# SiLU-gated product on one core: computed in place, 16 rows to a partition, products packed over rows already read

## The chip, the core and the metric

One core of a Trainium2 chip runs the kernel alone. The metric is device time in microseconds (us) of one execution, as the median of several runs. DVE is VectorE, ACT is ScalarE, SP is SyncE. DMA transfers are issued from two queues, SP's and ACT's, and both are carried out by the core's 16 DMA engines.

## The reference

The input x is float32 of shape 32 x 512 x 2048: 16384 rows of 2048 numbers (8 KiB a row, 134.22 MB). Each row is cut into two halves of 1024, and the output (67.11 MB) is

```python
half_dim = x.shape[-1] // 2
x1, x2 = (x[..., :half_dim].copy(), x[..., half_dim:].copy())
silu_x1 = x1 * (1 / (1 + np.exp(-x1)))
return (silu_x1 * x2).astype(np.float32)
```

Nothing is summed over rows or columns: it is an elementwise stream, two numbers in for one out.

## The kernel before

The rows are cut into 16 tiles of 128 partitions x 8 rows. In a tile a partition takes 8 neighbouring rows, 64 KiB in one piece of memory. `load(i)` (L82, issued on SP) brings a whole tile into `xt`, from a pool of two buffers of 64 KiB a partition. `silu` (L86, on ACT) reads the first halves of the rows and writes a second tile, `ot`, from a pool of two buffers of 32 KiB a partition. `mul` (L93, on DVE) multiplies `ot` in place by the second halves of `xt`. The store (L112, issued on ACT) sends `ot` out, 32 KiB a partition in one piece. The four buffers take 192 KiB of a partition.

The order is written out by hand (`manual_schedule`); waits are put in by the framework from what each instruction reads and writes. Tiles 0 and 1 are loaded ahead; the first load is moved in front of the program's first barrier. After the store of tile i has been queued, `load(i + 2)` is queued on SP. It goes into the buffer that tile i was read from, so it waits for the multiply of tile i. SiLU of tile i writes the output buffer that tile i - 2 left from, so it waits for the store of tile i - 2.

Three places differ from the rest:
- Tile 0 is computed in four chunks of two rows (`KC_EDGE`), and its store is cut into the five pieces of `OPENING`: every fourth partition's first two rows, and so on, growing from 256 KiB to 2 MiB.
- Tile 15, the last, is computed in two chunks of four rows (`KS`) and stored in two pieces (L120).
- L146 is the end of the program: barriers and waits for the last stores.

A transfer is carried out as one packet per partition, and each of the 16 DMA engines takes 8 of the 128 partitions. A DMA engine takes packets in turn from the two queues as long as both have some.

Of the kernel before, what the change touches and what calls it, by code (L numbers as in the profile page):

```python
# [1 line left out]

# [4 lines left out]


def issue_ahead_of_the_first_barrier(nc):

    head, body = nc.main_func.blocks[:2]
    load = next(ins for ins in body.instructions if type(ins).__name__ == "InstDMACopy")
    at = next(
        j for j, ins in enumerate(head.instructions)
        if ins.engine == load.engine and type(ins).__name__ == "InstDrain"
    )
    body.instructions = [ins for ins in body.instructions if ins.name != load.name]  # L20
    head.instructions = head.instructions[:at] + [load] + head.instructions[at:]


@with_exitstack
def kernel(
    ctx: ExitStack,
    tc: tile.TileContext,
    x: bass.AP,
    out: bass.AP,
):  # L30

    nc = tc.nc
    P = nc.NUM_PARTITIONS

    x_flat = x.flatten_outer_dims()  # L40
    out_flat = out.flatten_outer_dims()
    num_rows, in_cols = x_flat.shape
    half = in_cols // 2
    dt = x_flat.dtype

    K = 8
    KC_EDGE = 2
    KS = 4
    OPENING = [
        (slice(0, None, 4), slice(0, 2)),  # L50
        (slice(2, None, 4), slice(0, 4)),
        (slice(2, None, 4), slice(4, None)),
        (slice(0, None, 4), slice(2, None)),
        (slice(1, None, 2), slice(None)),
    ]
    PLAN = [K] * (num_rows // (P * K))

    in_pool = ctx.enter_context(tc.tile_pool(name="in_pool", bufs=2))
    out_pool = ctx.enter_context(tc.tile_pool(name="out_pool", bufs=2))

    plan = []
    row = 0
    for k in PLAN:
        plan.append((row, k))
        row += P * k
    assert row == num_rows
    n_tiles = len(plan)

    def view(flat, i):
        row0, k = plan[i]  # L70
        return flat[row0:row0 + P * k].rearrange("(p k) d -> p k d", k=k)

    nc.at_finalize(issue_ahead_of_the_first_barrier)


    ctx.enter_context(tc.manual_schedule())

    loaded = {}

    def load(i):  # L80
        xt = in_pool.tile([P, K, in_cols], dt, name="xt")
        nc.sync.dma_start(out=xt[:, :plan[i][1], :], in_=view(x_flat, i))  # L82
        loaded[i] = xt

    def silu(ot, xt, c, ce):
        nc.scalar.activation(  # L86
            out=ot[:, c:ce, :],
            in_=xt[:, c:ce, :half],
            func=mybir.ActivationFunctionType.Silu,
        )  # L90

    def mul(ot, xt, c, ce):
        nc.vector.tensor_mul(  # L93
            out=ot[:, c:ce, :],
            in0=ot[:, c:ce, :],
            in1=xt[:, c:ce, half:],
        )

    load(0)
    load(1)  # L100
    for i in range(n_tiles):
        xt = loaded.pop(i)
        ov = view(out_flat, i)
        ot = out_pool.tile([P, K, half], dt, name="ot")
        if i < n_tiles - 1:
            kc = KC_EDGE if i == 0 else K
            for c in range(0, K, kc):
                silu(ot, xt, c, c + kc)
                mul(ot, xt, c, c + kc)

            for ps, ks in OPENING if i == 0 else [(slice(None), slice(None))]:
                nc.scalar.dma_start(out=ov[ps, ks], in_=ot[ps, ks])  # L112
            if i + 2 < n_tiles:
                load(i + 2)
            continue
        for c in range(0, K, KS):
            silu(ot, xt, c, c + KS)
            mul(ot, xt, c, c + KS)
        for c in range(0, K, KS):
            nc.scalar.dma_start(out=ov[:, c:c + KS], in_=ot[:, c:c + KS])  # L120


# [1 line left out]
_INS = ['x']  # L124
_OUTS = [((32, 512, 1024), 'float32')]


# [23 lines left out]
```

## Time and profile before

| | |
|---|---|
| time, median of 3 runs | 470.3 us (470.26 to 470.54) |
| span of the profiled execution, first to last instruction | 468.4 us |
| lying around the span (median less span) | 1.9 us |
| HBM read / written | 134.22 MB / 67.11 MB |
| DVE busy | 139.3 us, 20 multiplies |
| ACT busy | 114.1 us, 20 SiLUs and one table load |
| SiLU / multiply of a whole tile (128 x 8192) | 7.03 us / 8.69 us |
| SiLU / multiply of two rows (128 x 2048) | 1.90 us / 2.29 us |

The span is measured by the profiler within one execution; the time of a run holds what lies around it too. No separate time of the profiled execution is given, so its span stands beside the median of the runs. The profile names idle time by what ended it ("<-DMA out_dram<-ot": the engine waited for a store of `ot` to land). A chain of waits is followed back from the last instruction. Besides the page, the trace holds a record of each DMA packet, with its queue, size, start and duration; times of packets below are counted from the start of the span as well.

### The profile page before, as it was taken

Reading aid. Unit: us, or ns where it says so; the run is one execution under the profiler, and the core shown is the slowest. Engines: PE = TensorE matmul, PEld = TensorE weight load, DVE = VectorE, ACT = ScalarE, POOL = GpSimd, SP = SyncE. Lnnn points to the kernel's source line nnn. Section 1 sums busy time; section 2 is a strip of 40 time slices with the busy share of each in tenths; the row PEclk is TensorE's granted clock in tenths of the full one; section 3 lists DMA queues with packets and bytes.
Section 4 is the critical chain, followed back from the end, with each engine's and each line's share of the span. In section 5 each row is a group of like instructions: output and inputs, shape, how many; then the busy total and the mean of one; then the engine's idle time right before and its main releaser. Section 6 shows DMA issues by size and latency. Waiting matters only on the chain.

```text
span 468.4 us, 185 instructions
## 1 busy us (share of the span) xinstructions
DVE 139.3 (30%) x20; ACT 114.1 (24%) x21; POOL 0.2 (0%) x4
## 2 busy tenths in 40 slices
DVE  0070600704207042070520605116061150602543
ACT  1142305005050050601406014060230602306060
POOL 0000000000000000000000000000000000000000
DMA  9899999999999999999999999899999899999998
GB/s 442 364 470 425 448 403 403 493 403 403 448 465 431 403 442 409 493 403 414 437 448 448 403 448 465 386 448 439 411 493 442 372 439 493 403 448 403 428 423 358
DMA packets 4880, 201.33 MB, mean 430 GB/s; under 512 B 592, under 2 KB 592, under 8 KB 592
## 3 DMA queue, kind: packets, MB, share of 16 engines
q1 hardware_dynamic: 2304, 134.22, 66.4%
q10 hardware_dynamic: 2576, 67.11, 33.2%
HBM read 134.22 MB, written 67.11 MB: 430 GB/s over the span
## 4 chain that ended last, share of the span: by engine, by line
DMA 72%; DVE 14%; ACT 11%; DVEq 1%; issue 0%
DMA out_dram<-ot 63%; DVE ot L93 14%; ACT ot L86 11%; DMA xt<-in_x_dram 9%; DVEq L146 1%
## 5 line engine op out<-in xcount | busy, mean ns | idle before, releaser
L93 DVE TENSOR_TENSOR ot<-ot,xt 128x8192 f32<-128x8192 f32 (+2 forms) x20 | 139.3, 6983 | 321.1 <-ACT ot L86 321.1
L86 ACT ACTIVATE ot<-xt 128x8192 f32<-128x8192 f32 (+2 forms) x20 | 112.8, 5661 | 340.2 <-DMA out_dram<-ot 305.8
L86 ACT ACT_TABLE_LOAD x1 | 1.3, 1283 | 0.8 <-PEq L135 0.8
L135 POOL MEMSET const-bfloat16-1.0<- 128x1 bf16 x1 | 0.1, 102 | 0.0
L135 POOL MEMSET const-uint8-127<- 128x1 uint8 x1 | 0.1, 102 | 0.0
L135 POOL MEMSET const-float32-1.0<- 128x1 f32 x1 | 0.1, 99 | 0.0
L135 POOL MEMSET const-float32-0.0<- 128x1 f32 x1 | 0.1, 98 | 0.2 <-issue 0.2
## 6 DMA issues: line engine op xcount, KB each, us to landing
out_dram<-ot ACTq DMA_DIRECT2D x14, 4096.0 KB, 42.2
out_dram<-ot ACTq DMA_DIRECT2D x3, 2048.0 KB, 6.9
out_dram<-ot ACTq DMA_DIRECT2D x2, 512.0 KB, 17.6
out_dram<-ot ACTq DMA_DIRECT2D x1, 768.0 KB, 28.2
xt<-in_x_dram SPq DMA_DIRECT2D x16, 35.1
out_dram<-ot ACTq DMA_DIRECT2D x1, 256.0 KB, 11.3
```

The costliest lines, as they stand in the source:

```text
L86: nc.scalar.activation(out=ot[:, c:ce, :], in_=xt[:, c:ce, :half], func=mybir.ActivationFunctionType.Silu,)
L93: nc.vector.tensor_mul(out=ot[:, c:ce, :], in0=ot[:, c:ce, :], in1=xt[:, c:ce, half:],)
L135: nc = _bacc.Bacc("TRN2", target_bir_lowering=False, num_devices=1)
L146: with _tile.TileContext(nc) as tc:
```

## The change

Tiles are taken in pairs. A partition now takes 16 neighbouring rows (128 KiB in memory), and there are 8 pairs. The first 8 rows of each partition are loaded into `a` (two buffers of 64 KiB), the other 8 into `b` (one buffer of 64 KiB): 192 KiB as before, and no output buffers. SiLU writes over the first halves that it reads. The multiply writes its products packed, over the front of `a`: `o` is a view of `a` as 16 rows of 1024. The products of a's own rows go to o's rows 0 to 7, those of b's rows to o's rows 8 to 15. A whole pair leaves as one store of 64 KiB a partition.

The half `a` is computed whole, the half `b` in four chunks of two rows. The loads are queued on SP as a(0), b(0), a(1), and then, after each pair's store, b(j+1) and a(j+2). b(j+1) goes where b(j) was read from, so it waits for the last multiply of b(j). a(j+2) goes where o of pair j leaves from, so it waits for every store of pair j.

The stores: pair 0 in five pieces (`OPENING`, now up to 64 KiB a partition), pairs 1 to 4 whole, pair 5 in two halves of the partitions (`HALVES`, even and odd), pair 6 as the rows of `a` and then the rows of `b`, pair 7 as the rows of `a` and then two quarters. In the changed kernel the loads of `a` are at L74, those of `b` at L79, SiLU at L83, the multiply at L88 and the stores at L96.

```diff
-    K = 8
-    KC_EDGE = 2
-    KS = 4
+    K = 8
+    KB = 2
+    PAIR = 2 * K
...
+    WHOLE = [(slice(None), 0, PAIR)]
+    HALVES = [(slice(0, None, 2), 0, PAIR), (slice(1, None, 2), 0, PAIR)]
     OPENING = [
-        (slice(0, None, 4), slice(0, 2)),
-        (slice(2, None, 4), slice(0, 4)),
-        (slice(2, None, 4), slice(4, None)),
-        (slice(0, None, 4), slice(2, None)),
-        (slice(1, None, 2), slice(None)),
+        (slice(0, None, 4), 0, 2),
+        (slice(2, None, 4), 0, 4),
+        (slice(2, None, 4), 4, PAIR),
+        (slice(0, None, 4), 2, PAIR),
+        (slice(1, None, 2), 0, PAIR),
     ]
...
-    in_pool = ctx.enter_context(tc.tile_pool(name="in_pool", bufs=2))
-    out_pool = ctx.enter_context(tc.tile_pool(name="out_pool", bufs=2))
+    a_pool = ctx.enter_context(tc.tile_pool(name="a_pool", bufs=2))
+    b_pool = ctx.enter_context(tc.tile_pool(name="b_pool", bufs=1))
...
+    x_of = x_flat.rearrange("(n p k) d -> n p k d", p=P, k=PAIR)
+    out_of = out_flat.rearrange("(n p k) d -> n p k d", p=P, k=PAIR)
+    a_of, b_of = {}, {}
+    def load_a(j):
+        a = a_pool.tile([P, K, in_cols], dt, name="a")
+        nc.sync.dma_start(out=a, in_=x_of[j, :, :K])
+        a_of[j] = a
+    def load_b(j):
+        b = b_pool.tile([P, K, in_cols], dt, name="b")
+        nc.sync.dma_start(out=b, in_=x_of[j, :, K:])
+        b_of[j] = b
+    def compute(t, o, r0, c, ce):
         nc.scalar.activation(
-            out=ot[:, c:ce, :],
-            in_=xt[:, c:ce, :half],
+            out=t[:, c:ce, :half],
+            in_=t[:, c:ce, :half],
             func=mybir.ActivationFunctionType.Silu,
         )
         nc.vector.tensor_mul(
-            out=ot[:, c:ce, :],
-            in0=ot[:, c:ce, :],
-            in1=xt[:, c:ce, half:],
+            out=o[:, r0 + c:r0 + ce, :],
+            in0=t[:, c:ce, :half],
+            in1=t[:, c:ce, half:],
         )
+    def store(j, o, pieces):
+        for ps, r, re in pieces:
+            nc.scalar.dma_start(out=out_of[j, ps, r:re], in_=o[ps, r:re])
+    load_a(0)
+    load_b(0)
+    load_a(1)
+    for j in range(n_pairs):
+        a, b = a_of.pop(j), b_of.pop(j)
+        o = a.rearrange("p k (h d) -> p (k h) d", h=2)
+        last = j == n_pairs - 1
+        split = j >= n_pairs - 2
+        compute(a, o, 0, 0, K)
+        if split:
+            store(j, o, [(ALL, 0, K)])
+        for c in range(0, K, KB):
+            compute(b, o, K, c, c + KB)
+        if last:
+            store(j, o, [(ALL, K, K + K // 2), (ALL, K + K // 2, PAIR)])
+            break
+        if split:
+            store(j, o, [(ALL, K, PAIR)])
+        else:
+            store(j, o, OPENING if j == 0 else HALVES if j == n_pairs - 3 else WHOLE)
+        load_b(j + 1)
+        if j + 2 < n_pairs:
+            load_a(j + 2)
```

More of the change, by code (lines that the diff above doesn't have):

```diff
@@ L46 @@
     K = 8
-    KC_EDGE = 2
-    KS = 4
-    OPENING = [
-        (slice(0, None, 4), slice(0, 2)),
-        (slice(2, None, 4), slice(0, 4)),
-        (slice(2, None, 4), slice(4, None)),
-        (slice(0, None, 4), slice(2, None)),
-        (slice(1, None, 2), slice(None)),
-    ]
-    PLAN = [K] * (num_rows // (P * K))
-    in_pool = ctx.enter_context(tc.tile_pool(name="in_pool", bufs=2))
-    out_pool = ctx.enter_context(tc.tile_pool(name="out_pool", bufs=2))
[L61 to L71, printed above, removed]
+    KB = 2
+    PAIR = 2 * K
+    n_pairs = num_rows // (P * PAIR)
+    assert n_pairs * P * PAIR == num_rows
+    WHOLE = [(slice(None), 0, PAIR)]
+    HALVES = [(slice(0, None, 2), 0, PAIR), (slice(1, None, 2), 0, PAIR)]
+    OPENING = [
+        (slice(0, None, 4), 0, 2),
[3 more added lines that the diff above has]
+        (slice(1, None, 2), 0, PAIR),
+    ]
@@ L73 @@
+    ALL = slice(None)
+    a_pool = ctx.enter_context(tc.tile_pool(name="a_pool", bufs=2))
+    b_pool = ctx.enter_context(tc.tile_pool(name="b_pool", bufs=1))
     nc.at_finalize(issue_ahead_of_the_first_barrier)
     ctx.enter_context(tc.manual_schedule())
[L78 to L85, printed above, removed]
+    x_of = x_flat.rearrange("(n p k) d -> n p k d", p=P, k=PAIR)
@@ L89, in silu @@
             func=mybir.ActivationFunctionType.Silu,
         )
-    def mul(ot, xt, c, ce):
         nc.vector.tensor_mul(
-            out=ot[:, c:ce, :],
-            in0=ot[:, c:ce, :],
-            in1=xt[:, c:ce, half:],
-        )
[L99 to L120, printed above, removed]
+            out=o[:, r0 + c:r0 + ce, :],
```

## The prediction

> **What bounds the kernel now.** I read the page first, for who is busy.
>
> ```profile
> span 468.4 us, 185 instructions
> ...
> DVE 139.3 (30%) x20; ACT 114.1 (24%) x21; POOL 0.2 (0%) x4
> ...
> DMA  9899999999999999999999999899999899999998
> ...
> q1 hardware_dynamic: 2304, 134.22, 66.4%
> q10 hardware_dynamic: 2576, 67.11, 33.2%
> ```
>
> The two compute engines are busy for 30% and 24%. The two DMA queues, loads (q1) and stores (q10), together hold the 16 DMA engines for 66.4 + 33.2 = 99.6% of the span: 311.0 and 155.5 us. So the bound is the DMA engines' own time, and the only room is 0.4% of 468.4 us, about 2 us. Nothing can make this kernel much faster; what can be lost is continuity. In the packet records, every engine takes its packets back to back, one per partition and transfer: 64 KiB of load in 2.418 us, 32 KiB of store in 1.213, 16 KiB in 0.611, 8 KiB in 0.309. From about 1.9 us after the span's start to its last microsecond no engine pauses for more than 0.1 us.
>
> Then the timeline, at both ends, for the latencies that a pause would be made of.
>
> ```profile
> 21.75 5.51 ACT L86 ACTIVATE ot<-xt 128x2048 f32<-128x2048 f32 x3 [19.70 <-DMA xt<-in_x_dram]
> ...
> 26.02 0.55 ACTq L112 DMA_DIRECT2D out_dram<-ot  x1
> ...
> 32.62 0.33 SPq L82 DMA_DIRECT2D xt<-in_x_dram  x1
> ...
> 439.57 0.34 ACTq L112 DMA_DIRECT2D out_dram<-ot  x1
> 448.01 7.12 ACT L86 ACTIVATE ot<-xt 128x4096 f32<-128x4096 f32 x2 [17.20 <-DMA out_dram<-ot]
> 451.66 8.76 DVE L93 TENSOR_TENSOR ot<-ot,xt 128x4096 f32<-128x4096 f32 x2 [12.13 <-ACT ot L86]
> 456.12 4.67 ACTq L120 DMA_DIRECT2D out_dram<-ot  x2
> ```
>
> Three numbers come out. (a) The first load is issued at 0.00 and its SiLU starts at 21.75, while its eight packets per engine need 8 x 2.418 = 19.34: a load put on drained queues costs 2.41 us beyond its bytes, about 0.38 of it notice (the last packet of a store ended at 447.62, the SiLU waiting for it started at 448.01). (b) The first of the last two stores is issued at 456.12, and its packets start at 456.97: 0.85 us from issue to packet when an engine has just run dry. (c) Four chunks of two rows need 32.62 - 21.75 = 10.87 us from a landed load to an issue behind the last multiply; two chunks (the second store at 28.22) need 6.47.
>
> Last, the chain and the SP queue's waits: who waits for stores today.
>
> ```profile
> DMA out_dram<-ot 63%; DVE ot L93 14%; ACT ot L86 11%; DMA xt<-in_x_dram 9%; DVEq L146 1%
> ```
>
> ```profile
> SPq L82 <- DVE ot L93: 301.6, 14, 23.0
> SPq L82 <- DMA xt<-in_x_dram: 102.9, 14, 20.6
> ```
>
> The chain runs through stores only because SiLU waits for a free output buffer. A load never waits for a store: it waits for the multiply that frees its input buffer (301.6 us in 14 waits), and at that time the next load is already queued. That is why neither queue runs dry.
>
> **The change, part by part.**
>
> *Compute.* Each pair has one SiLU of 7.03, one multiply of 8.69, and four chunks of 1.9 and 2.29 on its second half: ACT 8 x (7.03 + 7.6) = 117 us, DVE 8 x (8.69 + 9.14) = 143 us, against 114 and 139. Both have two thirds of each 58 us pair free, so I cost the extra at nothing; in place, the operands' sizes are the same. If that cover were gone it would be 3 to 4 us.
>
> *Bytes and packets.* Bytes do not change. Store packets per engine fall from 140 to 92 (opening 12, four whole stores 8 each, halves 8, split pairs 16 and 24). Two of 32 KiB cost 2.426 us, one of 64 KiB 2.418: 8 ns each. Packets overlap their neighbours by 3 ns (a tile's period is 29.00 us, its packets sum to 29.05), so 48 x 5 ns, a gain of 0.3 us. The bound: 48 x 8 ns, 0.4.
>
> *The new wait.* Load a(j+2) reuses the buffer that store j leaves from, so on SP it waits for a whole store to land, and b(j+2) stands behind it. On ACT the stores wait as before; behind them stand SiLUs of loads that land later. What matters is whether the load queue runs out before store j has landed.
>
> *Steady state: hidden.* Store j starts 0.38 + 10.87 + 0.85 = 12.1 us after b(j) has landed, while a(j+1) loads. Five of its packets are through by then and one or two more go ahead (the store issued at 26.02 started at 31.02, behind a packet of 28.3). The engines then alternate one store, one load packet, and a transfer's completion write takes a turn too (the before trace shows two loads or two stores in a row at exactly those places). Store j has 9 turns; loads left are one or two packets of a(j+1), eight of b(j+1) and two completions, 11 or 12. So two or three load packets, 4.8 to 7.2 us, remain when the store lands, and the next load needs 1.3 to 2.4. Free, with at least 2.4 us to spare.
>
> *First pair: not hidden.* a(0), b(0), a(1) are queued at once, b(0) lands at 21.4 + 19.3 = 40.7. The opening store is in five pieces: 12 packets and 5 completions, 17 turns. Its first two pieces need only the first half's product, but stand on ACT behind b(0)'s SiLUs: issued near 45, on the engines near 48; the rest follows at 40.7 + 0.4 + 10.9 = 52. From 48 the loads have five packets of a(1), eight of b(1) and two completions, 15 turns. So loads run out first, by one or two store packets, and a(2) may not be issued until the last piece has landed. The next store needs b(1)'s chunks and comes at about 106. So both queues drain. When: 32 load packets (77.4 us), 19.4 us of store, 2.0 us of start: 98.8, or up to 0.8 more, since loads beside the first small stores took 2.5 to 2.75 us in the before trace. The pause is notice plus restart: at least 0.38 + 0.03 + 0.85 = 1.3 us (row b, a store), at most 2.4 (row a, a load, but the program's first). Neither is nearer, so the middle: **1.9 us**, once. It ends the program that much later, because all else is bytes.
>
> *The tail.* Stores after b(7): the first quarter needs 0.38 + 6.47 + 0.85 = 7.7 us. By the same turns, six or seven packets of the preceding half store (1.213 each, 7.3 or 8.5 us) are still queued. A pause of 0.4 us or none; I take none. The last quarter needs 12.1 us, and 7.3 + 4.9 are queued.
>
> *Sum.* 1.9 - 0.3 + 0 = +1.6 us on the profiled span, 468.4 to 470.0. The median of the runs, 470.3, lies 1.9 us above the span for what is around it; that does not change. 470.3 + 1.6 = **471.9 us**.
>
> *A rule that speaks against the change.* In the before trace partitions are read at a pitch of 64 KiB and written at 32 KiB, and all packets but the opening's run at 2.418 and 1.213 us; the change doubles both pitches, and no row shows it for long transfers, but the opening stores (every fourth partition, 128 KiB apart) ran at the usual 0.309 and 0.611 us. The Trainium skill, "DMA: Bandwidth & Descriptors", section "Latency and other measured facts", says that large power-of-two pitches between partitions' rows slow HBM copies: 207 GB/s at 512 KiB where 214 is full. If that 3.3% reached the loads here, an estimate from that page would be 311 x 0.033, some 10 us more; this trace shows none of it.
>
> **The rivals.**
>
> *The pause is hidden (not slower).* If the opening pieces finish at least one 64 KiB packet earlier in the order of turns, a(2) is issued while b(1) still loads. It decides at two turns: the margin is 15 against 17. For it: ACT may issue the first pieces earlier than 45. Against: they cannot come before b(0) lands, and an earlier start brings the ends level rather than reversed. Time: 470.3 - 0.3 = 470.0, no change.
>
> *Faster.* Both the pause and the 0.8 us of slow loads beside the small first stores go: 470.3 - 0.3 - 0.8 = 469.2. Nothing points to it.
>
> *Longer pitch slows packets (much slower).* One per cent on each packet is 4.7 us: 475. Against: the 128 KiB opening stores above.
>
> *The pause recurs.* If a store of 64 KiB packets gets less than its turn, the load queue drains in pairs 1 to 5 also: 5 x 1.9 more, 481. Against: 2.4 us to spare and a fair alternation in the before trace.
>
> **How the numbers follow.** Forecast 0.72, hidden 0.11, faster 0.05, longer pitch 0.08, recurring 0.04. Around the forecast: pause 1.3 to 2.4, packets -0.4 to -0.3, tail 0 to 0.4, opening -0.8 to +0.4. The ends that I keep are 1.3 - 0.4 - 0.8 = +0.1 and 2.4 - 0.3 + 0.4 + 0.4 = +2.9: 470.3 rounded down to 470.2 to take in part of the hidden case, and 473.2. A measurement here tells 0.2%, 0.94 us, from no change. The hidden case and the low corner of the forecast fall within it, so: faster 0.05, same 0.17, slower 0.78.
>
> **What would show it.** Right: one wait of SP for out, ending at 99 to 100, then one pause of 1.3 to 2.4 us in which both queues are empty, seen as one lower digit in the DMA row near a fifth of the span; 64 KiB packets still at 2.418; the other a loads issued 4 to 8 us before the b load ahead of them lands; last SiLU group near 451. Wrong: a DMA row without a gap and a span under 468.8 (hidden), shares of q1 above 311 us (pitch), or gaps at each 58 us (recurring).

## The result, and the profile after

The changed kernel takes 483.3 us (median of 6 runs, 481.5 to 483.8) against 470.3 us: a ratio of 1.0252, 95% interval 1.0225 to 1.0280. I had forecast slower, but by 1.6 us and not by 13.0. The profiled execution took 483.4 us with a span of 481.6, 13.2 us more than the span before. Some executions of a kernel come out over 1.5% longer than its fastest; the ratios here and below leave these out.

The page of the changed kernel (busy tenths of the DMA engines in 40 slices of 12 us; then the two queues' packets, MB and share of 16 engines' span):

```profile
span 481.6 us, 203 instructions
...
DMA  9998989969999999999999999999999999999978
...
q1 hardware_dynamic: 2304, 134.22, 65.9%
q10 hardware_dynamic: 1728, 67.11, 32.3%
```

One slice, 96 to 108 us, is down to six tenths: the forecast pause. But the shares do not fall as a pause of 1.9 us would make them. 65.9% of 481.6 us is 317.4 us of load packets, against 311.0 before: the same 2304 packets with the same bytes took 6.4 us longer on each engine. That part was not in the forecast.

The SP queue's waits of the changed kernel (us in total, times, longest), then its timeline around the pause and at the end (start, us, engine, line, operation):

```profile
SPq L74 <- DMA out_dram<-a: 270.6, 9, 43.5
```

```profile
41.16 1.91 ACT L83 ACTIVATE b<-b 128x2048 f32<-128x2048 f32 x1 [12.32 <-DMA b<-in_x_dram]
41.17 1.20 ACTq L96 DMA_DIRECT2D out_dram<-a  x2
...
52.02 1.81 ACTq L96 DMA_DIRECT2D out_dram<-a  x3
...
102.15 7.31 ACT L83 ACTIVATE b<-b 128x2048 f32<-128x2048 f32 x4 [30.33 <-DMA b<-in_x_dram]
102.24 0.33 SPq L74 DMA_DIRECT2D a<-in_x_dram  x1
...
113.02 0.36 ACTq L96 DMA_DIRECT2D out_dram<-a  x1
...
462.52 7.31 ACT L83 ACTIVATE b<-b 128x2048 f32<-128x2048 f32 x4 [21.37 <-DMA b<-in_x_dram]
...
468.99 4.74 ACTq L96 DMA_DIRECT2D out_dram<-a  x2
```

b(1) and the opening store have landed at the same time, at 101.7, and only then is a(2) issued, at 102.24. The last b half lands at 462.2 and its first store follows 6.47 us after its SiLU has begun, as row (c) had it.

Stretches of the changed kernel (length, then busy time of DVE, ACT and POOL, clock, DMA share, GB/s):

```profile
96.00:104.00 8.00, 0.00 (x0) 1.85 (x2) 0.00 (x0) 1.00 0.72 270
...
114.00:122.00 8.00, 0.00 (x0) 0.00 (x0) 0.00 (x0) 1.00 0.88 319
122.00:172.00 50.00, 14.58 (x4) 14.34 (x5) 0.00 (x0) 1.00 1.00 435
```

The second row is what I had no term for. Nothing computes, both queues have work, store 1 has just been issued, and the rate is 319 GB/s; in the 50 us behind it it is 435. In the packet records all 16 engines have one load packet there, begun at 116.0 to 116.5, that takes 3.3 to 3.9 us instead of 2.418; behind it their first packet of store 1 follows.

From the packet records I made a ledger for each run, in us per engine (sums over all packets divided by 16; "load excess" is the duration of the load packets above 2.418 us for 64 KiB, 1.213 for 32 KiB; idle times are those of the engines between packets; the records name no engine, and an engine's packets are told by each beginning where the one before ended):

| kernel | load excess | idle 4 to 120 us | idle 120 to 440 us | idle from 440 us to the last packet |
|---|---|---|---|---|
| before | 1.42 | 0.02 | 0.05 | 0.18 |
| changed | 7.79 | 4.04 | 0.35 | 2.61 |

The differences, 6.4 + 4.0 + 0.3 + 2.4 us, with 0.2 us less of store packets, make 12.9 of the 13.2 us. The rest, 0.3, I leave unassigned.

### The profile page after: what moved, and what is told of

The parts are those of the page before. It is cut to its first block, busy times and chain, and to the rows that moved or that the text cites. A ratio compares the mean times of both kernels' runs of the same rounds, so it can differ in the third digit from the quotient of the medians.

```text
span 481.6 us, 203 instructions
## 1 busy us (share of the span) xinstructions
DVE 140.7 (29%) x40; ACT 116.0 (24%) x41; POOL 0.2 (0%) x4
## 3 DMA queue, kind: packets, MB, share of 16 engines
q1 hardware_dynamic: 2304, 134.22, 65.9%
## 4 chain that ended last, share of the span: by engine, by line
DMA 70%; DVE 12%; another core or an unknown queue 9%; ACT 5%; DVEq 0%; ACTq 0%; issue 0%
DMA b<-in_x_dram 38%; DMA out_dram<-a 19%; DMA a<-in_x_dram 13%; DVE a L88 12%; ACT a L83 3%; ACT b L83 2%; DVEq L146 0%; ACTq L96 0%; ACTq L83 0%
## 5 line engine op out<-in xcount | busy, mean ns | idle before, releaser
L88 DVE TENSOR_TENSOR a<-a 128x8192 f32<-128x8192 f32 x8 | 69.5, 8692 | 187.0 <-ACT a L83 187.0
L88 DVE TENSOR_TENSOR a<-b 128x2048 f32<-128x2048 f32 x32 | 71.2, 2286 | 145.6 <-ACT b L83 145.6
L83 ACT ACTIVATE b<-b 128x2048 f32<-128x2048 f32 x32 | 58.5, 1897 | 199.9 <-DMA b<-in_x_dram 199.9
L83 ACT ACTIVATE a<-a 128x8192 f32<-128x8192 f32 x8 | 56.2, 7029 | 153.2 <-DMA a<-in_x_dram 153.2
```

Source lines behind the costliest of these rows:

```text
L83: nc.scalar.activation(out=t[:, c:ce, :half], in_=t[:, c:ce, :half], func=mybir.ActivationFunctionType.Silu,)
L88: nc.vector.tensor_mul(out=o[:, r0 + c:r0 + ce, :], in0=t[:, c:ce, :half], in1=t[:, c:ce, half:],)
```

## The experiments

**Which parts count: pair 1 split (e1_split1), all pairs split (e2_splitall), the old order at the new pitch (e3_pitch), the old order with small load packets (e4_load32).**

Pair 1 in two row halves, so that the store queue has work while a(2) waits:

```diff
-        split = j >= n_pairs - 2
+        split = j == 1 or j >= n_pairs - 2
```

> The changed kernel, with pair 1 stored in two row halves (the first right behind the multiply of its a half) instead of whole; all else as changed. The store queue then has work at 99 us, while a(2) waits for the opening store. Theory A (continuity: the 13.2 us more of span are the pause at 99 to 103 us, 4.0 us and 0.75 us of slow first packets behind it; about 5.3 us of load packets that run above 2.418 us when a store starts on an empty store queue; and about 2 us of idle engines before the last two stores): the pause goes and with it one store start, so 5 to 6 us less, 477 to 479 us. Theory B (addresses: loads are slower because a partition's rows lie 128 KiB apart): the pause goes, the slow load packets stay just as many, 478 to 480 us, and they are not tied to store starts. If the pause were the whole loss: 470 to 472 us.

Measured: 476.2, 478.2 and 479.7 us, and 483.6 in the profiled run (ratio of the first three 1.0153, 1.0112 to 1.0194). The pause is gone: 0.16 us of idle time from 4 to 120 us against 4.04. The slowed loads are not: the load excess of the profiled run is 9.97 us, where theory A had it fall. That run took 4 to 7 us longer than the other three, which left no packet records, so how much those lost to slowed loads is not shown. By their times, against 483.3, the pause was worth about 5 us, and was not the whole.

All pairs in row halves:

```diff
-        split = j >= n_pairs - 2
+        split = True
```

> The changed kernel, with every pair stored in two row halves of 32 KiB a partition, each behind its own multiply (pair 0 too, in place of its five pieces); loads and their 128 KiB pitch as changed. Store packets are 32 KiB against 64 KiB of load, so the store queue should never run empty. Theory A: no pause, no store starts, so load packets near 2.418 us throughout (sum above nominal 1 to 2 us an engine, as before the change); what is left is a wait of 1.8 to 2.5 us before the last two stores; 471.5 to 474 us. Theory B: the slow load packets stay, 475 to 479 us.

Measured: 472.75 us (472.1 to 473.3; ratio 1.0044, 1.0026 to 1.0063). Its page, and its timeline at the end:

```profile
span 470.9 us, 200 instructions
...
DMA  9899999998999999999999999999999999999998
```

```profile
452.43 7.31 ACT L83 ACTIVATE b<-b 128x2048 f32<-128x2048 f32 x4 [21.86 <-DMA b<-in_x_dram]
...
458.90 4.74 ACTq L96 DMA_DIRECT2D out_dram<-a  x2
```

In place computing, the 16-row layout, the two-row chunks and a(j+2)'s wait for a store are all still there, and 10.6 of the 13.0 us are gone. The load excess is 2.83 us; from 110 us on no load packet is slow. What is left is two places: 1.08 us of load and 0.4 us of store excess at 100 to 109 us, where the load queue has just run empty and a(2) is issued beside running stores, and 0.98 us of idle before the last stores.

The kernel before, with the pitch of the changed one:

```diff
-        row0, k = plan[i]
-        return flat[row0:row0 + P * k].rearrange("(p k) d -> p k d", k=k)
+        j, t = divmod(i, 2)
+        pair = flat[j * P * 2 * K:(j + 1) * P * 2 * K]
+        return pair.rearrange("(p t k) d -> t p k d", t=2, k=K)[t]
```

> The kernel before, with its order, chunks, buffers and packet sizes, but its tiles laid out as halves of 16-row groups: a partition's loads lie 128 KiB apart (64 before) and its stores 64 KiB apart (32 before). Theory A: nothing changes, 470.0 to 470.7 us. Theory B: several us slower, 475 to 482 us.

Measured: 470.32 us (10 runs; ratio 0.9993, 0.9972 to 1.0014), load excess 1.43 us. Theory B is out: 128 KiB between a partition's loads and 64 KiB between its stores cost nothing. The Trainium skill's rule on large power-of-two pitches ("DMA: Bandwidth & Descriptors", "Latency and other measured facts") does not reach down to these pitches; no run here tried its own, 512 KiB and more.

The kernel before, with loads of 32 KiB a partition:

```diff
-        nc.sync.dma_start(out=xt[:, :plan[i][1], :], in_=view(x_flat, i))
+        for c in range(0, K, 4):
+            nc.sync.dma_start(out=xt[:, c:c + 4, :], in_=view(x_flat, i)[:, c:c + 4])
```

> The kernel before, each load issued as two loads of 4 rows (32 KiB a partition), stores as before. Load and store packets now are of one size, so stores get every second turn and half of the engines' time beside loads instead of a third: the store queue runs empty in each tile and starts anew 14 times beside loads, as in the changed kernel, at the old pitch and with 32 KiB store packets. By the order of turns alone the end has a pause of about 4.6 us (the stores have run out when the last load lands), and 128 more packets an engine cost 0.6 us: 475 to 476 us with load packets at their nominal 1.213 us (theory B, and theory C: that only 64 KiB store packets disturb loads). Theory A: on top of that 0.3 to 1.1 us of slowed load packets at each of the 14 starts, 479 to 490 us.

Measured: 474.1 to 474.4 us in three runs, 479.6 in the profiled one (ratio 1.0101, 1.0045 to 1.0158). The store queue did run empty in every tile, but the load excess is only 3.33 us for 14 starts. Theory A as I had put it, that a store starting on an empty queue costs 0.3 to 1.1 us each time, fails here: it came to that at two of the 14 starts, with 0.45 and 0.95 us.

**Is a start enough? The remedy (e6_fix), bare streams with 64 KiB and 32 KiB stores (m1_starts64, m2_starts32), and 32 KiB stores in the changed kernel (e5_rows).**

All pairs split, with two edits more:

```diff
-        compute(a, o, 0, 0, K)
+        for c in range(0, K, KB if j == 0 else K):
+            compute(a, o, 0, c, c + (KB if j == 0 else K))
...
-            store(j, o, [(ALL, K, K + K // 2), (ALL, K + K // 2, PAIR)])
+            store(j, o, [(ALL, r, r + KB) for r in range(K, PAIR, KB)])
```

> All pairs stored in row halves, as in the run with every pair split (472.75 us), with two more edits. Pair 0's a half is computed in chunks of two rows, so that its first store is issued at about 32.6 us instead of 37.6 and the store that a(2) waits for lands before the load queue runs out. The last b half is stored in four pieces of two rows, each behind its own multiply, so that the first is issued 1.9 us earlier. Theory A' (what costs is a queue that runs empty and starts anew beside the other one, whichever of the two it is, about 1 us of slowed packets each time, and idle engines): the slow packets at 100 to 109 us (1.45 us) and the idle 1 us before the last stores go, 470.0 to 471.0 us. Rival (in place computing or the two-row chunks cost something of their own): it stays at 472 to 473 us.

Measured: 470.87 us against 470.57 of the kernel before in the same set (ratio 0.9997, 0.9981 to 1.0013). Its timeline:

```profile
33.28 0.37 ACTq L96 DMA_DIRECT2D out_dram<-a  x1
...
95.28 0.33 SPq L74 DMA_DIRECT2D a<-in_x_dram  x1
102.74 7.31 ACT L83 ACTIVATE b<-b 128x2048 f32<-128x2048 f32 x4 [22.11 <-DMA b<-in_x_dram]
```

The first store leaves at 33.28, and a(2) is now issued 7.5 us before b(1)'s SiLU instead of just behind it. Load excess 1.60, idle 0.01 and 0.07 us up to 440. So computing in place is as fast as the kernel before once the queues are kept fed, and not faster: the bytes bound both.

The bare stream (the loop of the changed kernel replaced; `s` is a constant tile; the second differs only in storing the first 8 rows):

```diff
+    for i in range(2 * n_pairs):
+        xt = tiles.pop(i)
+        nc.scalar.activation(
+            out=s[:, 0, 0:1] if i % 2 else w,
+            in_=xt[:, 0, 0:1],
+            func=mybir.ActivationFunctionType.Silu,
+        )
+        if i % 2:
+            nc.scalar.dma_start(out=out_of[i // 2], in_=s)
+        if i + 2 < 2 * n_pairs:
+            tiles[i + 2] = load(i + 2)
```

> A bare stream with the changed kernel's transfers: 16 loads in two buffers at the 128 KiB pitch and 8 stores of 64 KiB a partition, of a constant tile; of the computing only one element per partition and load is left, so that store j is issued when load 2j+1 has landed. No load waits for a store, so the load queue never runs empty, but each of the first 7 stores starts on an empty store queue beside loads. Without a cost of starting: 468.4 + about 1.5 us of pause before the last store, - 0.3 us, so some 471.5 us with load packets at 2.418 us. Theory A': 0.5 to 1.3 us of slowed load packets at most of the 7 starts, 475 to 480 us. If the slowed packets need the compute engines' work at the same time: none.

> The bare stream with stores of 32 KiB a partition: only the first 8 of a pair's 16 rows are stored, so half of the output is left out. Bytes take 309.5 + 77.6 us an engine, and without a cost of starting the time is some 393 to 394 us. Theory A' (the start costs, not the store's packet size): the 7 starts cost 0.5 to 1.3 us each as with 64 KiB, 397 to 402 us. Theory C (only store packets of 64 KiB disturb loads): nothing, 393 to 394 us.

Measured: 477.2 us (476.4 and 478.1) and 397.5 us. Both times lie in the range of theory A', but not for its reason. At the first start the loads lost 0.96 and 1.01 us; at the other six 0.01 to 0.13 us with 64 KiB and 0.03 to 0.42 with 32 KiB. Most of what cost time was that the engines drifted apart. In the 64 KiB stream the first load landed on its last engine 0.65 us after its first, the 15th load 14.1 us, the last load 6.5 us; and the last store could not be issued before the slowest engine was done, 6.1 us of idle time per engine. So a start on an empty queue is not sufficient, nor does it take store packets of 64 KiB: theories A' and C both fail.

Pairs 1 to 4 with both row halves stored behind the last multiply:

```diff
-    WHOLE = [(slice(None), 0, PAIR)]
+    WHOLE = [(slice(None), 0, K), (slice(None), K, PAIR)]
```

> The changed kernel with pairs 1 to 4 stored as two stores of 32 KiB a partition, both behind the pair's last multiply (one store of 64 KiB before). By the order of turns each store of a pair now needs 18 turns where 11 or 12 of the loads are left, so the load queue runs dry in pairs 0 to 4, and a(j+2) waits for the store: five pauses of 1.3 to 4 us where the changed kernel has one, each followed by a slow first load packet of about 0.75 us. Theory A': 488 to 500 us. Theory C (64 KiB store packets are what costs): fewer slowed load packets, faster than the changed kernel, below 481 us.

Measured: 490.9 to 492.8 us, 499.0 in the profiled run (ratio 1.0436, 1.0398 to 1.0474). The page:

```profile
span 497.2 us, 212 instructions
...
DMA  9999999989999799998998969898799999999987
```

In this profiled run, 6 to 8 us above the other three, the notches stand 60 us apart, one for each of pairs 0 to 4; the idle time from 120 to 440 us is 14.9 us, and the load excess 10.06 us. Stores of 32 KiB are not a remedy by themselves: with twice the turns they land too late, and the loads wait. The count of turns was right here.

**What a start needs beside it: the changed kernel's waits without its computing, with a long and a short chain (m3_late, m4_early), and a free load queue with the long chain (m5_late_free).**

In each loop `act(w, w)` stands between the landed b half and the store, six times or twice:

```diff
+        act(a[:, 0, 0:1], a[:, 0, 0:1])
+        act(w[:, 0:1], b[:, 0, 0:1])
+        for _ in range(6):
+            act(w, w)
+        act(a[:, 0, 0:1], w[:, 0:1])
+        nc.scalar.dma_start(out=out_of[j], in_=a.rearrange("p k (h d) -> p (k h) d", h=2))
...
-        for _ in range(6):
+        for _ in range(2):
```

> The changed kernel's transfers, buffers and waits (b(j+1) after b(j) has been read, a(j+2) after store j has landed, stores of 64 KiB a partition, all whole), without its computing: what is stored is x as it was loaded, so the output is not the product. Between a landed b(j) and store j stands a chain of six small activations on a scratch tile, 11 to 12 us, as long as the changed kernel's chunks. By the order of turns a(j+2) is then ready 2 to 4 us before the load queue would run out. Theory D (a store that starts on an empty queue slows loads by about 1 us when the load queue has only just been handed its next transfer, and hardly when that was queued long before): 0.5 to 1.3 us of slowed load packets at most of stores 1 to 6, as in the changed kernel, 484 to 489 us. Theory E (the slowed loads need the multiplies and SiLUs of the changed kernel beside them or before them): below 0.2 us at a start but the first, 482 to 483 us.

> The same with two small activations in the chain instead of six: store j is issued 4 to 5 us after b(j) has landed, and a(j+2) is ready some 10 us before the load queue would run out. Theory D: below 0.2 us of slowed loads at each start but the first, 475 to 477 us. If the slowing belongs to a start on an empty store queue alone, or to the buffers and waits: as much as with six activations, 0.5 to 1.3 us a start, 479 to 484 us.

The bare stream with the long chain ahead of each store, where a load only waits for the load that had its buffer:

```diff
+            for _ in range(6):
+                nc.scalar.activation(out=v, in_=v, func=mybir.ActivationFunctionType.Silu)
+            nc.scalar.activation(out=s[:, 0, 1:2], in_=v[:, 0:1], func=mybir.ActivationFunctionType.Silu)
             nc.scalar.dma_start(out=out_of[i // 2], in_=s)
```

> The bare stream with 64 KiB stores of a constant tile (no load waits for a store, each load is queued a whole transfer ahead), now with the chain of six small activations between a landed load and its store, 12 us. Stores so start on an empty queue as late as in the run with the long chain, but the load queue always has its next transfer long before. Theory D (the margin with which the load queue is handed its next transfer decides): below 0.2 us of slowed loads at each start but the first. Theory F (the place decides: a store that starts 12 us into a load, whatever the loads wait for): 0.4 to 1.5 us at most starts, as with the long chain before. The time of the whole says little, since the last store is issued 12 us after the last load: 484 to 492 us.

Measured: 498.7, 484.7 and 490.7 us. From the timelines, one pair each of the changed kernel, of the long and of the short chain: the issue of a(4), the first read of the landed b(3), the store behind it.

```profile
218.53 0.33 SPq L74 DMA_DIRECT2D a<-in_x_dram  x1
223.34 7.31 ACT L83 ACTIVATE b<-b 128x2048 f32<-128x2048 f32 x4 [27.59 <-DMA b<-in_x_dram]
...
234.21 0.36 ACTq L96 DMA_DIRECT2D out_dram<-a  x1
```

```profile
216.26 0.33 SPq L74 DMA_DIRECT2D a<-in_x_dram  x1
221.03 0.20 ACT L103 ACTIVATE w<-b 128x1 f32<-128x1 f32 x1 [31.78 <-DMA b<-in_x_dram]
...
233.14 0.34 ACTq L115 DMA_DIRECT2D out_dram<-a  x1
```

```profile
210.24 0.33 SPq L74 DMA_DIRECT2D a<-in_x_dram  x1
220.61 0.20 ACT L103 ACTIVATE w<-b 128x1 f32<-128x1 f32 x1 [26.77 <-DMA b<-in_x_dram]
...
224.96 0.34 ACTq L115 DMA_DIRECT2D out_dram<-a  x1
```

The lead, from a's issue to the read of the landed b, is 4.8 us in the first two and 10.4 in the third. With the load excess around each start (packets that begin from 6 us ahead of the first store packet to 2.5 us behind it):

| run | lead of the next load, us | load excess at each start after the first, us |
|---|---|---|
| changed kernel, stores 1 to 5 | none, 7.3, 4.8, 4.2, 4.9 | 1.13, 0.02, 0.76, 1.23, 0.54 |
| long chain, stores 1 to 6 | 4.8, 2.8, 4.8, 3.2, 4.4, 2.7 | 0.43, 1.15, 1.57, 1.11, 1.39, 0.93 |
| short chain, stores 1 to 6 | 12.1, 12.1, 10.4, 11.2, 12.1, 11.0 | 0.04, 0.01, 0.04, 0.15, 0.01, 0.06 |
| free load queue, long chain, stores 1 to 6 | a whole load or more | 0.19, 0.00, 0.01, 0.04, 0.04, 0.08 |

In these runs, where both queues move packets of 64 KiB, leads under 5 us go with 0.4 to 1.6 us lost, leads above 7 with 0.2 at most. It needs no computing beside it but single activations (the long chain), and it isn't the place of the start within a load (the free queue, same place, at most 0.19 us). Theories E and F fall, D stands: a store that starts on an empty queue slows the loads when the load queue has only just been handed its next transfer. A long lead is not a safeguard in every case: with 32 KiB stores m2_starts32 lost up to 0.42 us with a whole load of lead, and with 32 KiB loads the two starts of e4_load32 that lost 0.45 and 0.95 us had leads of 20 us. Those are not explained. The whole times of the three were above what I expected (484 to 489, 475 to 477) or at its upper end, for the reason that the first streams had shown: the last load landed 3.5, 9.4 and 15.2 us apart on the engines, and the last store waited for the slowest, 16, 13 and 22 us of idle time from 440 us on.

Why a short lead slows a load packet that is served many microseconds later is open. Nor was the excess of 1.15 us at 384 to 386 us in the changed kernel explained, where a store joins stores that are still running.

## Why the prediction was wrong, point by point

**The bound, the bytes, compute.** Right. DVE and ACT took 140.7 and 116.0 us, off the path. Store packets took 0.2 us less in all (0.3 forecast, from 48 x 5 ns = 0.24).

**The new wait and the pause of the first pair.** Right in place and mechanism: the loads ran out, the opening store landed at 101.7, one drop in the DMA row; the pause comes once in the run. The first two pieces were issued at 41.17 and on the engines at 45.2, not near 45 and 48: ACT issued them with the first of b(0)'s SiLUs, not behind the last. The loads still ran out first, by one store packet on each engine. The size of the pause was taken at 1.9 us and is 4.0 us idle, and the loads behind it took another 0.75 us. The missing part is a step I did not make: I followed one engine for all 16. Fifteen engines had ended their last packet by 99.6; one ended at 101.71, because five of its load packets between 66 and 94 us, out of step with the others, had lost 2.3 us in sum. A transfer has landed when its slowest engine is done. From 101.71 the notice took 0.53 and the restart 0.96 us, inside the bounds of 1.3 to 2.4.

**"Steady state: hidden."** Half right, and the main error. No engine ran dry between 120 and 440 us to speak of (0.35 us), as the count of turns said. But "free, with at least 2.4 us to spare" was wrong: short of running dry, a lead of 4 to 5 us already cost 0.5 to 1.2 us of slowed loads at each start of a store, and no lead, at the first, 1.13. The sum had "all else is bytes" at 2.418 us a packet. That number came from a trace in which neither queue ever ran empty after the opening, so it could not show what a restart costs. The one row that hinted at it, the loads of 2.5 to 2.75 us beside the first small stores, I carried over as a constant of the opening instead of asking what else would start a queue anew. The load excess of 6.4 us more is half of the 13: 3.7 us stand at the five starts, 0.75 behind the pause, 1.15 at 384 to 386 us.

**The tail.** I took none of 0 to 0.4 us; it was 2.4 us. Again the spread: b(7) landed on the first engine at 459.4 and on the last at 462.2, fifteen engines had sent their backlog by 468.2, and the quarter store issued at 468.99 reached them at 469.8.

**The rivals.** The longer pitch was wrong (e3_pitch). The sign that I had set for it, more than 311 us of load packets, did appear, with 317.4: it tells that loads are slow, not why. The pause that recurs came true in e5_rows, not here. The slowing without a pause was not among them. Of the range's terms, each was bounded by rows of a run that had none of the states the change makes; the upper end, 473.2, should have held the price of five restarts at the 0.3 us of the opening's slow packets at least, and of a landing spread of one whole packet, 2.4 us, at both places where a wait decides.

## What to carry to other kernels

In a kernel that only streams, keep both DMA queues from running empty: queue each load a whole transfer ahead, and cut stores so that the share of turns they get matches the share of bytes. Buffers that are shared between loads and stores make the load wait for the slowest engine of a whole store; check the lead of that load, and count on it costing before it reaches zero. When costing a change, ask of each duration in which state of the queues it was measured.

## What the runs showed of the hardware that I had not expected

- The first store of a run, started beside loads, slowed each engine's loads by about 1 us in the five runs without computing (0.93 to 1.01 us), with packets of 64 and of 32 KiB, issued at 41.6 to 53.5 us.
- Engines left step in the runs whose store queue ran empty: a load's landing, spread over 0.44 us in the kernel before, spread over up to 15 us with the short chain and with the free load queue. The Trainium skill, "DMA: Bandwidth & Descriptors", section "Why a DMA increments its semaphore by 16 and not by 1", says that a transfer's engines finish independently and that only the full count means landed; these spreads are what that can cost.
- Away from a start, with work in both queues, the changed kernel moved 435 GB/s from 122 to 172 us, with 64 KiB packets of both kinds in turn.
